# Batch normalisation on one core: the stream of 8 MB tiles moves from two hardware DMA queues to GpSimd's one software queue, one packet per DMA engine

## The chip, the cores and the metric

The kernel runs on one core of a Trainium2 chip. The metric is the device time of one launch in microseconds (us): the median of the runs was 2484.65 us. The core has a vector engine (VectorE, "DVE" in the profile), a scalar engine (ScalarE, "ACT"), GpSimd ("POOL"), TensorE (not used here) and SyncE ("SP"). Data moves between the device memory and the on-chip memory by DMA; the core has 16 DMA engines, and each transfer here is shared out over all of them.

## The reference

The input x has shape 32 x 256 x 128 x 128 in 32-bit floats (537 MB). Each channel is scaled and shifted with its own four parameters:

```python
def reference(x, gamma, beta, running_mean, running_var):
    eps = 1e-5
    mean = running_mean.reshape(1, -1, 1, 1)
    var = running_var.reshape(1, -1, 1, 1)
    gamma = gamma.reshape(1, -1, 1, 1)
    beta = beta.reshape(1, -1, 1, 1)
    return gamma * (x - mean) / np.sqrt(var + eps) + beta
```

So every element is read once, multiplied by a number of its channel, added to another, and written once.

## The kernel before

The 256 channels are two blocks of 128, one channel to a partition. With 32 images this gives 64 tiles (NT), each of 128 partitions x 16384 floats: 128 rows of 65,536 bytes, 8 MB in all. Three buffers of that size (NBUF = 3) hold tiles in turn: tile i is loaded into buffer i mod 3, worked on in place, and stored from there.

**Head.** SP issues the left half of tile 0 (L88), then four small broadcast loads with the parameters (L91), then the right half of tile 0 (L95), then the whole tiles from 1 on (L102). VectorE and ScalarE turn the parameters into one scale and one shift for each channel (L107 to L125).

**A tile's work.** VectorE takes columns 0 to 14335 of a tile in two instructions (2560 columns, then 11776, both L130) and counts each in the semaphore `vdone`; ScalarE takes the last 2048 columns (L141) and counts in `adone`. Tile 0 is cut at its half instead, so that VectorE can begin when the left half is there. In the last tile ScalarE takes 7168 columns, so that both engines end sooner.

**Order of transfers.** Loads are issued by SP and go to one hardware queue, q1; stores are issued by ScalarE (L154) and go to another, q10. From tile 3 on, SP waits until the earlier store out of the same buffer has landed (`stored`, L101) and until VectorE has done the first piece of the tile before (`vdone`, the wait on L102). ScalarE issues the store of tile i behind its own part of tile i, and begins its part only when VectorE is done with tile i (L162) and the store of tile i - 1 has landed (L165). So at most one store is under way until near the end, while a load runs beside it. Each transfer has its own semaphore per buffer (`loaded`, `stored`), which rises by 16, one for each DMA engine.

**End.** SP waits for the last store of each buffer (L172).

Of the kernel before, what the change touches and what calls it, by code (L numbers as in the profile page):

```python
# [8 lines left out]
NBUF = 3  # L9
# [3 lines left out]
VCOLS = 14336  # L13
VLAST = 9216


@with_exitstack
def kernel(
    ctx: ExitStack,
    tc: tile.TileContext,  # L20
    x: bass.AP,
    gamma: bass.AP,
    beta: bass.AP,
    running_mean: bass.AP,
    running_var: bass.AP,
    out: bass.AP,
):
    nc = tc.nc
    eps = 1e-5
    f32 = mybir.dt.float32  # L30

    N, C, H, W = x.shape
    P = nc.NUM_PARTITIONS
    assert C % P == 0
    NCB = C // P
    HW = H * W
    NT = N * NCB
    B = 32
    NQ = P // B
    NE = 16  # L40
    NPAR = 4

    xr = x.rearrange("n (cb p) h w -> (n cb) p (h w)", p=P)
    outr = out.rearrange("n (cb p) h w -> (n cb) p (h w)", p=P)

    params = ctx.enter_context(tc.tile_pool(name="params", bufs=1))
    data = ctx.enter_context(tc.tile_pool(name="data", bufs=1))
    bufs = [data.tile([P, HW], f32, name=f"t{s}", tag=f"t{s}") for s in range(NBUF)]
    rows = params.tile([B, NPAR * C], f32, name="rows", tag="rows")
    turned = params.tile([B, NPAR * C], f32, name="turned", tag="turned")  # L50
    par = params.tile([P, NPAR, NCB], f32, name="par", tag="par")
    eps_t = params.tile([P, 1], f32, name="eps_t", tag="eps")
    std_t = params.tile([P, NCB], f32, name="std_t", tag="std")
    rstd_t = params.tile([P, NCB], f32, name="rstd_t", tag="rstd")
    scale_t = params.tile([P, NCB], f32, name="scale_t", tag="scale")
    ms_t = params.tile([P, NCB], f32, name="ms_t", tag="ms")
    shift_t = params.tile([P, NCB], f32, name="shift_t", tag="shift")

    loaded = [tc.alloc_semaphore(f"loaded{s}") for s in range(NBUF)]
    stored = [tc.alloc_semaphore(f"stored{s}") for s in range(NBUF)]
    early = tc.alloc_semaphore("early")
    vdone = tc.alloc_semaphore("vdone")
    adone = tc.alloc_semaphore("adone")
    fetched = tc.alloc_semaphore("fetched")
    vec = tc.alloc_semaphore("vec")
    act = tc.alloc_semaphore("act")

    with tc.tile_critical():  # L70
        count = [0]

        def step(inst, sem=None, value=None):

            if sem is not None:
                inst._wait_ge(sem, value)
            elif count[0]:
                inst._wait_ge(vec, count[0])
            inst.then_inc(vec, 1)
            count[0] += 1  # L80
            return count[0]

        left, right = slice(0, HW // 2), slice(HW // 2, HW)
        last = NT - 1

        nc.sync.dma_start(out=bufs[0][:, left], in_=xr[0][:, left]).then_inc(early, 16)  # L88
        zeroed = step(nc.vector.memset(rows[:], 0.0))  # L89
        for r, ap in enumerate((running_var, gamma, beta, running_mean)):  # L90
            inst = nc.sync.dma_start(out=rows[0:NE, r * C : (r + 1) * C], in_=ap.partition_broadcast(NE))  # L91
            if r == 0:
                inst._wait_ge(vec, zeroed)
            inst.then_inc(fetched, 16)
        nc.sync.dma_start(out=bufs[0][:, right], in_=xr[0][:, right]).then_inc(loaded[0], 16)  # L95
        for i in range(1, NT):
            s, turn = i % NBUF, i // NBUF


            if turn:  # L100
                nc.sync.wait_ge(stored[s], 16 * turn)  # L101
            inst = nc.sync.dma_start(out=bufs[s][:], in_=xr[i]).then_inc(loaded[s], 16)  # L102
            if turn:
                inst._wait_ge(vdone, 2 * (i - 1) + 1)


        step(nc.vector.memset(eps_t[:], eps))  # L107
        step(nc.vector.transpose(out=turned[:], in_=rows[:]), fetched, 16 * NPAR)  # L108

        blocks = turned.rearrange("p (rc q b) -> p rc q b", q=NQ, b=B)  # L110
        flat = par.rearrange("p r cb -> p (r cb)")
        for q in range(NQ):
            placed = step(nc.vector.tensor_copy(out=flat[q * B : (q + 1) * B], in_=blocks[:, :, q, 0]))  # L113
        var_t, gamma_t, beta_t, mean_t = (par[:, r] for r in range(NPAR))
        nc.scalar.activation(  # L115
            out=std_t[:],
            in_=var_t,
            func=mybir.ActivationFunctionType.Sqrt,
            bias=eps_t[:],
            scale=1.0,  # L120
        )._wait_ge(vec, placed).then_inc(act, 1)
        step(nc.vector.reciprocal(out=rstd_t[:], in_=std_t[:]), act, 1)  # L122
        step(nc.vector.tensor_mul(out=scale_t[:], in0=gamma_t, in1=rstd_t[:]))  # L123
        step(nc.vector.tensor_mul(out=ms_t[:], in0=mean_t, in1=scale_t[:]))  # L124
        ready = step(nc.vector.tensor_sub(out=shift_t[:], in0=beta_t, in1=ms_t[:]))  # L125
        nc.vector.wait_ge(vec, ready)

        def vector_part(i, first, end):
            t, cb = bufs[i % NBUF], i % NCB
            return nc.vector.tensor_scalar(  # L130
                out=t[:, first:end],
                in0=t[:, first:end],
                scalar1=scale_t[:, cb : cb + 1],
                scalar2=shift_t[:, cb : cb + 1],
                op0=mybir.AluOpType.mult,
                op1=mybir.AluOpType.add,
            ).then_inc(vdone, 1)

        def scalar_part(i, first):
            t, cb = bufs[i % NBUF], i % NCB  # L140
            return nc.scalar.activation(  # L141
                out=t[:, first:],
                in_=t[:, first:],
                func=mybir.ActivationFunctionType.Identity,
                bias=shift_t[:, cb : cb + 1],
                scale=scale_t[:, cb : cb + 1],
            ).then_inc(adone, 1)

        def landed(i):
            return loaded[i % NBUF], 16 * (i // NBUF + 1)  # L150

        def store(i):
            s = i % NBUF
            nc.scalar.dma_start(out=outr[i], in_=bufs[s][:])._wait_ge(adone, i + 1).then_inc(stored[s], 16)  # L154

        vector_part(0, 0, HW // 2)._wait_ge(early, 16)
        vector_part(0, HW // 2, VCOLS)._wait_ge(*landed(0))
        for i in range(1, NT):
            vector_part(i, 0, STEP)._wait_ge(*landed(i))
            vector_part(i, STEP, VLAST if i == last else VCOLS)  # L160
        for i in range(last):
            nc.scalar.wait_ge(vdone, 2 * (i + 1))  # L162
            inst = scalar_part(i, VCOLS)
            if i:
                inst._wait_ge(stored[(i - 1) % NBUF], 16 * ((i - 1) // NBUF + 1))  # L165
            store(i)
        scalar_part(last, VLAST)._wait_ge(*landed(last))
        nc.scalar.wait_ge(vdone, 2 * NT)
        store(last)

        for s in range(NBUF):
            nc.sync.wait_ge(stored[s], 16 * ((NT - s + NBUF - 1) // NBUF))  # L172


# [28 lines left out]
```

## Time and profile before

| quantity | value |
|---|---|
| median of 3 runs | 2484.65 us (2484.54 to 2486.47) |
| span of the profiled execution | 2483.3 us |
| VectorE busy | 508.8 us (20%) |
| ScalarE busy | 139.8 us (6%) |
| GpSimd busy | 0.2 us |
| read from and written to device memory | 536.94 MB and 536.87 MB |
| mean rate over the span | 432 GB/s |
| load of a whole tile, issue to landing (median) | 37.0 us |
| store of a whole tile, issue to landing (median) | 36.5 us |

The time of the runs is taken from outside the program, the span from its first to its last instruction; the difference is about 1.3 us. The instructions that issue DMAs or wait on semaphores are not counted as busy, so GpSimd, SP and most of ScalarE's work with queues is seen in the waits and in the timeline, not in the busy times. "Packets" are the pieces in which a DMA engine moves data: before, each row of a tile is one packet of 65,536 bytes, and each engine closes a transfer with a packet of 4 bytes that raises the semaphore.

### The profile page before, as it was taken

The numbers are of one execution on the slowest core, as the hardware profiler recorded it, in microseconds if no ns is written. First come the engines' busy times: TensorE is split into PE (matmuls) and PEld (weight loads), VectorE is DVE, ScalarE is ACT, GpSimd is POOL, SyncE is SP. The second block draws the span as 40 slices with busy tenths as digits, with TensorE's granted clock in tenths as the row PEclk, the third lists the DMA queues.
The fourth block names the chain that finished last, engine by engine and source line by source line (L and its number), as shares of the span: only waits on it lengthen the run. The fifth ranks groups of instructions, "written<-read, shape, count | busy, mean of one in ns | idle before, by whom it ended". The sixth has DMA issues, their size and how long they took to land.

```text
span 2483.3 us, 516 instructions
## 1 busy us (share of the span) xinstructions
DVE 508.8 (20%) x139; ACT 139.8 (6%) x66; POOL 0.2 (0%) x4
## 2 busy tenths in 40 slices
DVE  3122121221212212122121221212212122121220
ACT  0000000000000000000000000000000000000001
POOL 0000000000000000000000000000000000000000
DMA  9999999999999999999999999999999999999999
GB/s 415 430 439 434 428 436 436 435 433 430 432 433 438 430 432 433 435 424 437 437 428 436 438 436 429 437 435 430 436 437 436 430 437 435 429 437 435 433 433 408
DMA packets 18708, 1073.85 MB, mean 432 GB/s; under 512 B 2128, under 2 KB 2192, under 8 KB 2192
## 3 DMA queue, kind: packets, MB, share of 16 engines
q1 hardware_dynamic: 9488, 536.94, 50.1%
q10 hardware_dynamic: 9216, 536.88, 49.9%
q14 instruction: 4, 0.03, 0.0%
HBM read 536.94 MB, written 536.87 MB: 432 GB/s over the span
## 4 chain that ended last, share of the span: by engine, by line
DMA 93%; DVE 4%; another core or an unknown queue 1%; ACT 0%; issue 0%; SPq 0%; DVEq 0%
DMA t<-in_x_dram 93%; DVE t L130 4%; ACT t L141 0%; SPq L91 0%; DVE rows L89 0%; SPq L95 0%; DVE eps_t L107 0%; DVEq L198 0%; SPq L70 0%
## 5 line engine op out<-in xcount | busy, mean ns | idle before, releaser
L130 DVE TENSOR_SCALAR t<-t,scale_t,shift_t 128x11776 f32<-128x11776 f32 (+2 forms) x128 | 505.3, 3989 | 1930.4 <-DMA t<-in_x_dram 1930.2
L141 ACT ACTIVATE t<-t,shift_t,scale_t 128x2048 f32<-128x2048 f32 x64 | 138.2, 2159 | 2299.3 <-DMA out_dram<-t 2276.6
L108 DVE STREAM_TRANSPOSE turned<-rows 32x1024 f32<-32x1024 f32 x1 | 1.2, 1233 | 12.5 <-DMA rows<-in_running_mean_dram 12.5
L115 ACT ACT_TABLE_LOAD x1 | 1.3, 1283 | 0.9 <-SPq L70 0.9
L89 DVE MEMSET rows<- 32x1024 f32 x1 | 0.9, 912 | 1.2 <-SPq L70 1.2
L115 ACT ACTIVATE std_t<-par,eps_t 128x2 f32<-128x2 f32 x1 | 0.3, 296 | 14.7 <-DVE par L113 14.7
L113 DVE COPY par<-turned 32x8 f32<-32x8 f32 x4 | 0.6, 161 | 0.1
L122 DVE RECIPROCAL rstd_t<-std_t 128x2 f32<-128x2 f32 x1 | 0.2, 166 | 0.4 <-ACT std_t L115 0.4
L125 DVE TENSOR_TENSOR shift_t<-par,ms_t 128x2 f32<-128x2 f32 x1 | 0.2, 161 | 0.0
L124 DVE TENSOR_TENSOR ms_t<-par,scale_t 128x2 f32<-128x2 f32 x1 | 0.2, 161 | 0.0
L123 DVE TENSOR_TENSOR scale_t<-par,rstd_t 128x2 f32<-128x2 f32 x1 | 0.2, 160 | 0.0
L187 POOL MEMSET const-bfloat16-1.0<- 128x1 bf16 x1 | 0.1, 101 | 0.0
L187 POOL MEMSET const-uint8-127<- 128x1 uint8 x1 | 0.1, 101 | 0.0
L187 POOL MEMSET const-float32-0.0<- 128x1 f32 x1 | 0.1, 98 | 0.2 <-issue 0.2
L187 POOL MEMSET const-float32-1.0<- 128x1 f32 x1 | 0.1, 98 | 0.0
L107 DVE MEMSET eps_t<- 128x1 f32 x1 | 0.1, 59 | 0.1
## 6 DMA issues: line engine op xcount, KB each, us to landing
t<-in_x_dram SPq DMA_DIRECT2D x2, 4096.0 KB, 16.5
out_dram<-t ACTq DMA_DIRECT2D x64, 36.5
t<-in_x_dram SPq DMA_DIRECT2D x63, 37.0
rows<-in_running_var_dram SPq DMA_DIRECT2D x1, 16.0 KB, 11.3
rows<-in_gamma_dram SPq DMA_DIRECT2D x1, 16.0 KB, 11.1
rows<-in_beta_dram SPq DMA_DIRECT2D x1, 16.0 KB, 10.9
rows<-in_running_mean_dram SPq DMA_DIRECT2D x1, 16.0 KB, 11.3
```

Of the source, the lines that this page charges most:

```text
L89: zeroed = step(nc.vector.memset(rows[:], 0.0))
L107: step(nc.vector.memset(eps_t[:], eps))
L108: step(nc.vector.transpose(out=turned[:], in_=rows[:]), fetched, 16 * NPAR)
L113: placed = step(nc.vector.tensor_copy(out=flat[q * B : (q + 1) * B], in_=blocks[:, :, q, 0]))
L115: nc.scalar.activation(out=std_t[:], in_=var_t, func=mybir.ActivationFunctionType.Sqrt, bias=eps_t[:], scale=1.0,)._wait_ge(vec, placed).t ...
L122: step(nc.vector.reciprocal(out=rstd_t[:], in_=std_t[:]), act, 1)
L123: step(nc.vector.tensor_mul(out=scale_t[:], in0=gamma_t, in1=rstd_t[:]))
L124: step(nc.vector.tensor_mul(out=ms_t[:], in0=mean_t, in1=scale_t[:]))
L125: ready = step(nc.vector.tensor_sub(out=shift_t[:], in0=beta_t, in1=ms_t[:]))
L130: return nc.vector.tensor_scalar(out=t[:, first:end], in0=t[:, first:end], scalar1=scale_t[:, cb : cb + 1], scalar2=shift_t[:, cb : cb + 1 ...
L141: return nc.scalar.activation(out=t[:, first:], in_=t[:, first:], func=mybir.ActivationFunctionType.Identity, bias=shift_t[:, cb : cb + 1] ...
L187: nc = _bacc.Bacc("TRN2", target_bir_lowering=False, num_devices=1)
```

## The change

The two halves of tile 0 and the parameters stay on SP's queue. All other loads and all stores are issued by GpSimd, in the order: load 1, store 0, load 2, store 1, load 3, store 2, load 4 and so on. GpSimd's DMAs go to its one software queue, for which GpSimd itself writes the descriptors. With `single_packet=True` the eight rows that each DMA engine moves of a tile form one packet.

A store waits in GpSimd's queue for both parts of the work on its tile (`vdone` and `adone`). A load into a buffer used before waits for the store out of that buffer (`stored`). SP no longer waits for the work of VectorE, and ScalarE neither issues stores nor waits for VectorE or for an earlier store: it begins its part of a tile when the tile has landed. The right half of tile 0 has a semaphore of its own, `first`, so the counts of `loaded[0]` begin with tile 3. ScalarE gets one wait for the scale and shift, and the last waits move from SP to GpSimd.

```diff
-        nc.sync.dma_start(out=bufs[0][:, right], in_=xr[0][:, right]).then_inc(loaded[0], 16)
-        for i in range(1, NT):
+        nc.sync.dma_start(out=bufs[0][:, right], in_=xr[0][:, right]).then_inc(first, 16)
+
+        def load(i):
             s, turn = i % NBUF, i // NBUF
+            inst = nc.gpsimd.dma_start(out=bufs[s][:], in_=xr[i], single_packet=True).then_inc(loaded[s], 16)
             if turn:
-                nc.sync.wait_ge(stored[s], 16 * turn)
-            inst = nc.sync.dma_start(out=bufs[s][:], in_=xr[i]).then_inc(loaded[s], 16)
-            if turn:
-                inst._wait_ge(vdone, 2 * (i - 1) + 1)
+                inst._wait_ge(stored[s], 16 * turn)
+
+        def store(i):
+            s = i % NBUF
+            nc.gpsimd.wait_ge(vdone, 2 * (i + 1))
+            inst = nc.gpsimd.dma_start(out=outr[i], in_=bufs[s][:], single_packet=True)
+            inst._wait_ge(adone, i + 1).then_inc(stored[s], 16)
+
+        load(1)
+        for i in range(NT):
+            store(i)
+            if i + 2 < NT:
+                load(i + 2)
...
         nc.vector.wait_ge(vec, ready)
+        nc.scalar.wait_ge(vec, ready)
...
         def landed(i):
-            return loaded[i % NBUF], 16 * (i // NBUF + 1)
-
-        def store(i):
-            s = i % NBUF
-            nc.scalar.dma_start(out=outr[i], in_=bufs[s][:])._wait_ge(adone, i + 1).then_inc(stored[s], 16)
+            if i == 0:
+                return first, 16
+            return loaded[i % NBUF], 16 * (i // NBUF + (1 if i % NBUF else 0))
...
-        for i in range(last):
-            nc.scalar.wait_ge(vdone, 2 * (i + 1))
-            inst = scalar_part(i, VCOLS)
-            if i:
-                inst._wait_ge(stored[(i - 1) % NBUF], 16 * ((i - 1) // NBUF + 1))
-            store(i)
-        scalar_part(last, VLAST)._wait_ge(*landed(last))
-        nc.scalar.wait_ge(vdone, 2 * NT)
-        store(last)
+        for i in range(NT):
+            scalar_part(i, VLAST if i == last else VCOLS)._wait_ge(*landed(i))
 
         for s in range(NBUF):
-            nc.sync.wait_ge(stored[s], 16 * ((NT - s + NBUF - 1) // NBUF))
+            nc.gpsimd.wait_ge(stored[s], 16 * ((NT - s + NBUF - 1) // NBUF))
```

## The prediction

> **What bounds the kernel now.** First the page: the busy times, the DMA row, the queues and the chain that ended last.
>
> ```profile
> span 2483.3 us, 516 instructions
> ...
> DVE 508.8 (20%) x139; ACT 139.8 (6%) x66; POOL 0.2 (0%) x4
> ...
> DMA  9999999999999999999999999999999999999999
> ...
> q1 hardware_dynamic: 9488, 536.94, 50.1%
> q10 hardware_dynamic: 9216, 536.88, 49.9%
> ...
> DMA 93%; DVE 4%; another core or an unknown queue 1%; ACT 0%; issue 0%; SPq 0%; DVEq 0%
> ```
>
> No engine is busy over 20%, and the two queues' packets together fill 100.0% of the 16 DMA engines' span: the DMA engines are the bound. Next, three stretches cut out of the trace (length; busy VectorE, ScalarE and GpSimd; clock; DMA share; GB/s): loads alone in the head, 56 tiles in the middle, and the end, where mostly stores are left.
>
> ```profile
> 1.95:22.40 20.45, 7.12 (x12) 0.53 (x2) 0.00 (x0) 1.00 1.02 417
> ...
> 244.99:2408.90 2163.91, 442.74 (x111) 117.18 (x56) 0.00 (x0) 1.00 1.00 434
> ...
> 2441.87:2461.20 19.33, 5.27 (x2) 6.36 (x1) 0.00 (x0) 1.00 1.00 434
> ```
>
> The middle takes 2163.91/56 = 38.64 us for a load and a store, 16.777 MB, so 434 GB/s, 19.3 us for each transfer; the end has the same rate. The DMA share is 1.00 in all three: a queue alone keeps the engines as full as two do. Then the waits of SP's queue, and the head in order of time.
>
> ```profile
> SPq L101 <- DMA out_dram<-t: 1398.1, 61, 68.8
> SPq L102 <- DVE t L130: 985.0, 61, 16.2
> ```
>
> ```profile
> 18.04 4.55 DVE L130 TENSOR_SCALAR t<-t,scale_t,shift_t 128x8192 f32<-128x8192 f32 x1
> 23.85 3.48 DVE L130 TENSOR_SCALAR t<-t,scale_t,shift_t 128x6144 f32<-128x6144 f32 x1 [1.27 <-DMA t<-in_x_dram]
> 27.36 2.09 ACT L141 ACTIVATE t<-t,shift_t,scale_t 128x2048 f32<-128x2048 f32 x1 [10.23 <-DVE t L130]
> 29.49 0.37 ACTq L154 DMA_DIRECT2D out_dram<-t  x1
> 54.40 7.93 DVE L130 TENSOR_SCALAR t<-t,scale_t,shift_t 128x2560 f32<-128x2560 f32 x2 [27.07 <-DMA t<-in_x_dram]
> ```
>
> SP waits 2383.1 us in all, yet no DMA engine runs dry: those waits cost nothing, and dropping them gains nothing. In the head, tile 0 is worked on from 18.04 to 29.45 us while loads 1 and 2 keep the DMA engines full.
>
> So only three things can change the time: the cost of a packet, a hole in the DMA engines' work, and the cost of passing from one transfer to the next.
>
> **Packets, a gain.** The trace's records of single packets last 2.418 us for 65,536 bytes, 1.213 us for 32,768, 0.046 us for 1,024 and 0.009 us for 4. The first two differ by 1.205 us, so the bytes of a row take 2.410 us and 0.008 us is the packet's own. Successive records of an engine overlap by 0.004 us (a row begins every 2.414 us), so what a packet costs the engine is nearer 0.004 us. One packet for eight rows removes 7 of 8 in 63 loads and 64 stores: 127 x 7 = 889 per engine. At 0.004 us that is 3.6 us, at 0.008 us 7.1 us; if the price belongs to the row and not to the packet, nothing. I take 3.6, by the spacing, which is what fills the span. More than this can't come of it: a row's bytes keep their 2.410 us.
>
> **The steady state, nothing.** In the new order a store sits on the software queue ahead of the next load, so the two take turns, 19.3 us each. When load i lands, store i-1 starts. The work on tile i takes 8.0 us (54.40 to 62.33), so store i enters the queue 11 us before store i-1 ends, and behind it load i+1 is there already for another 19.3 us. Load i+2 waits for store i-1 and is queued behind store i in GpSimd's order; it is issued some 36 us before its turn. Every wait in GpSimd's order is over in time, so issue and description of a transfer are hidden unless they take over 11 us; the only rows are 0.34 us (SP and ScalarE issuing) and, as the other end, the 8.0 us for which VectorE works. Without that cover the price would be the excess times 64. Changing direction costs nothing in the rows: from 60 us on the records of each engine alternate between q1 and q10 at the same 2.414 us.
>
> **Taken away, nothing.** 63 loads, 64 stores and their waits leave SP's and ScalarE's queues. ScalarE's part now runs beside VectorE's, 2.09 us inside 8.0. At the end load 63, store 62 and store 63 follow each other; the last work (6.36 us, L141) lies under store 62 (19.3 us), as it lies under DMA now. The last waits only change engine.
>
> **The head, a loss.** Before, tile 0, load 1 and load 2 were on one queue in that order. Now load 2 is behind store 0 in GpSimd's queue, and load 1 starts beside tile 0 as a second queue. If an engine, once it has taken up load 1's packet, keeps to it for its eight rows, tile 0's rest comes after it, and by 2 + 2 x 19.3 + about 0.4 for the parameters = 41 us both are in and the queues are empty. Then come 0.5 us from the last packet of the right half to VectorE's start (23.35 to 23.85 before), 3.48 us for VectorE's second piece, and 1.0 us from an issue to its first packet (0.95 to 1.95 us for L88): 5.0 us. Row by row in turns, the halves of tile 0 also come last and the hole is the same. The parameters come later, but their work and VectorE's first piece (4.55 us) fit under the right half (9.6 us).
> One thing makes it longer. Load 1 is already there, so VectorE goes straight on to tile 1, 1.61 and 6.41 us, while GpSimd is to write the descriptors of store 0. No row shows GpSimd doing that beside VectorE. Bounds: no delay, 5.0; delay until VectorE has done both pieces, 13.0. I take a delay of the first piece, 1.6: 6.6 us, as GpSimd is ready before the second starts. The low end of the hole is 0: tile 0 complete before load 1's packets begin.
> The Trainium skill, page "SBUF — State Buffer", section "Who interferes with whom", speaks against the change here: an instruction of VectorE that streams through two ports locks GpSimd out for its whole length, and descriptors of GpSimd's DMAs are then late. The row that bears on it is L130's two shapes, 9216 columns more in 4.795 us, 0.52 ns a column. By the rule the hole would be the one of 6.6 or 13.0, by the plain rows 5.0.
>
> **From one transfer to the next, unknown.** Where one queue works alone (q1 at 23 us, between tile 0 and load 1; q10 at 2461 us, between the last two stores), the next row's record starts 6 ns after the 4-byte record that ends a transfer, with no gap: so 0 per boundary. The upper end is the largest stall that the trace has when a new transfer joins: at 32 us, when the first store starts, the load rows under way grow from 2.42 to between 2.74 and 3.64 us, some 0.8 us per engine (12.6 us summed over 16); over 127 boundaries 102 us. I take 0, as both queues of before showed it.
> The skill's page "DMA: Bandwidth & Descriptors", section "Anatomy of one DMA — SWDGE (gpsimd) path", gives each software DMA about 2.0 us beyond its bytes. If none of that overlapped, an estimate by that page is 127 x 2.0 = 254 us more; the records above say that for a hardware queue it overlaps wholly, and no run here shows the software queue.
>
> **Sum.** 2483.3 - 3.6 + 6.6 = 2486.3 us of span; the runs' median is 1.35 above the span, so 2487.7 us.
>
> **Rivals.**
> 1. VectorE holds up store 0 for both its pieces: hole 13.0, time 2484.65 - 3.6 + 13.0 = 2494.1. For it: the two instructions follow each other at 0.03 us. Against: GpSimd waits already when the first ends. It decides from a hole of 8.6 us.
> 2. Each boundary on the single queue costs something, since the same queue has to read, write and report with no second queue to fill in. From 2487.7, 2.0 us more (16 ns per boundary) make the kernel slower than the bound of measurement; 0.1 us each give 2500.4, 0.8 us 2589. For it: nothing covers it. Against: the records of 6 ns.
> 3. Faster: no hole, because tile 0 is through first, and 0.008 us per packet: 2484.65 - 7.1 = 2477.5; if the extra that load rows show over 2.418 us (64 us over 16 engines, 4.0 each, nearly all before 1141 us) also went as loads no longer meet stores, 2473.5. For it: the stores show almost no such extra. Against: both come late in the same mix with the same packets, so it isn't the mix.
> 4. The packets aren't merged: gain 0, 2491.3. Against: nothing in the trace speaks to it.
>
> **Chances.** A measurement of this kernel can tell about 0.2%, 5.0 us, from no change: 2479.7 to 2489.6. Forecast 0.35, with a range of its own of 2481 to 2489.6; rival 1 0.22, rival 2 0.18, rival 3 0.20, rival 4 0.05. Faster 0.20, same 0.35, slower 0.22 + 0.18 + 0.05 = 0.45. The range 2475 to 2505 leaves out a little of rival 3 and of rival 2 what lies above 0.14 us per boundary, some 0.15 in all.
>
> **What will show it.** Packets: 16 large ones per DMA transfer instead of 128, near 19.28 us each. Steady state: 38.58 us per tile, DMA share 1.00, GpSimd waiting for VectorE and for stores without gaps. Head: a DMA share near 0 for some 5 to 13 us from about 41 us, with store 0 issued after it and VectorE's tile 1 in the same stretch. If the share is below 1.00 in the middle, the boundary rival holds; a period over 38.64 us makes the prediction wrong, as does a head without the hole.

## The result, and the profile after

The changed kernel takes 2499.56 us (2498.44 to 2500.20) against 2485.52 us (2484.54 to 2486.47) for the kernel before in the same runs: 14.0 us or 0.58% longer, ratio 1.0058 with a 95% interval of 1.0046 to 1.0070. The forecast was 2487.7 us and no change that can be measured; the range of 2475 to 2505 holds the time. The span of the profiled execution is 2496.7 us, 13.3 us longer than before.

The page of the changed kernel: busy times, DMA row, queues, the chain that ended last, and the groups of GpSimd's issues (count, then busy time and mean duration).

```profile
span 2496.7 us, 460 instructions
...
DVE 508.7 (20%) x139; ACT 139.8 (6%) x66; POOL 74.5 (3%) x131
...
DMA  8999999999999999999999999999999999999998
...
q0 software_dynamic: 18288, 1065.36, 98.7%
q1 hardware_dynamic: 416, 8.45, 0.8%
...
another core or an unknown queue 90%; ACT 5%; DMA 3%; DVE 0%; issue 0%; POOL 0%; SPq 0%; DVEq 0%; POOLq 0%
...
L107 POOL DMA_DIRECT2D out_dram<-t x64 | 34.6, 541 | 1738.9 <-DVE t L140 1672.6
L100 POOL DMA_DIRECT2D t<-in_x_dram x63 | 39.6, 629 | 648.9 <-DMA out_dram<-t 647.9
```

The DMA engines are still the bound: both end slices of the DMA row are below 9, the 38 between are full. The software queue's 18288 packets are 16256 rows of 65,536 bytes and 2032 closing ones of 4 bytes, so each row is still a record of its own: the eight rows of an engine did not form one packet, against the title and the section on the change. One issue takes GpSimd some 0.54 us, hidden behind transfers of 19.3 us. The chain calls 90% of the span an unknown queue: most of the software queue's transfers get no name there, so this view tells nothing of the change, and the stretches and the timeline have to.

Three stretches of the changed kernel (columns as before: length; busy VectorE, ScalarE, GpSimd; clock; DMA share; GB/s): a gap in the head, 31 tiles in the middle, and the early part.

```profile
42.40:48.20 5.80, 5.39 (x3) 4.08 (x2) 1.32 (x2) 1.00 0.00 0
...
1218.93:2416.70 1197.77, 246.00 (x62) 64.94 (x31) 33.12 (x62) 1.00 1.00 434
140.00:600.00 460.00, 88.18 (x23) 23.93 (x12) 12.28 (x23) 1.00 1.00 432
```

In the head all 16 DMA engines stand still for these 5.8 us (0.00). The middle runs at 1197.77/31 = 38.64 us per tile, the same as before to the last digit. The early part is a little slower than the middle (432 against 434 GB/s; the kernel before has 433 in the same stretch). The timeline shows what happens in the gap (start, duration).

```profile
42.81 11.33 DVE L140 TENSOR_SCALAR t<-t,scale_t,shift_t 128x6144 f32<-128x6144 f32 x3 [1.38 <-DMA t<-in_x_dram]
46.88 1.06 POOL L107 DMA_DIRECT2D out_dram<-t  x1 [44.71 <-DVE t L140]
47.92 6.33 POOL L100 DMA_DIRECT2D t<-in_x_dram  x1
54.69 0.53 POOL L107 DMA_DIRECT2D out_dram<-t  x1 [0.44 <-issue]
```

The last data of tile 0 arrive at 42.3 us; VectorE's second piece lasts from 42.81 to 46.29, GpSimd begins store 0 at 46.88 and ends its issue at 47.94, and the store's first row starts at 48.5. Nothing else was queued in the meantime.

With the trace's records of single DMA packets the 13.3 us can be split fully. For each profile the table takes, per DMA engine (mean over 16): time without a packet in the head, the time by which rows last longer than 2.418 us, the time between an engine's own last packet and the last of all, and the time from that one to the end of the span. Two kernels of the experiments stand beside.

| us per DMA engine | before | changed | same order, hardware queue | loads 1 and 2 on SP's queue |
|---|---|---|---|---|
| no packet, up to 30 us | 0.2 | 0.3 | 0.2 | 0.3 |
| no packet, hole in the head | 0 | 6.5 | 0 | 0 |
| rows longer than 2.418 us | 4.1 | 7.5 | 4.2 | 4.2 |
| engines not ending together | 1.3 | 3.2 | 3.9 | 5.6 |
| last packet to end of span | 1.6 | 3.1 | 2.1 | 2.9 |
| sum over "before" | | 13.4 | 3.2 | 5.8 |
| span over "before" | | 13.3 | 3.1 | 5.8 |

The sums match the spans. In the changed kernel 109 of the 120 us of extra row time (summed over 16 engines) lie on the eighth row of a transfer: 96 on the eighth rows of loads, where an engine passes from a load to a store, and 13 on the eighth row of the first store, at 65 us, where it passes on to load 2. The eighth rows of all later stores have next to nothing. The two first passages, at 65 and 85 us, cost 0.8 and 1.0 us per engine (rows of up to 3.5 and 3.9 us), the next ones from a load to a store 0.1 to 0.4 us; from 1000 us on some 0.03 us are left on average.

### The profile page after: what moved, and what is told of

It reads as the page before. It is cut to its first block, busy times and chain, and to the rows that moved or that the text cites. A ratio compares the mean times of both kernels' runs of the same rounds, so it can differ in the third digit from the quotient of the medians.

```text
span 2496.7 us, 460 instructions
## 1 busy us (share of the span) xinstructions
DVE 508.7 (20%) x139; ACT 139.8 (6%) x66; POOL 74.5 (3%) x131
## 3 DMA queue, kind: packets, MB, share of 16 engines
q0 software_dynamic: 18288, 1065.36, 98.7%
## 4 chain that ended last, share of the span: by engine, by line
another core or an unknown queue 90%; ACT 5%; DMA 3%; DVE 0%; issue 0%; POOL 0%; SPq 0%; DVEq 0%; POOLq 0%
ACT t L151 5%; DMA t<-in_x_dram 3%; DVE t L140 0%; POOL out_dram L107 0%; SPq L92 0%; DVE rows L90 0%; DVE eps_t L116 0%; DVEq L199 0%; POOLq L106 0%; SPq L71 0%
## 5 line engine op out<-in xcount | busy, mean ns | idle before, releaser
L107 POOL DMA_DIRECT2D out_dram<-t x64 | 34.6, 541 | 1738.9 <-DVE t L140 1672.6
L100 POOL DMA_DIRECT2D t<-in_x_dram x63 | 39.6, 629 | 648.9 <-DMA out_dram<-t 647.9
```

What stands on the lines that cost most here:

```text
L100: inst = nc.gpsimd.dma_start(out=bufs[s][:], in_=xr[i], single_packet=True).then_inc(loaded[s], 16)
L107: inst = nc.gpsimd.dma_start(out=outr[i], in_=bufs[s][:], single_packet=True)
```

## The experiments

**The flag off.** `single_packet=True` is dropped in both calls:

```diff
-            inst = nc.gpsimd.dma_start(out=bufs[s][:], in_=xr[i], single_packet=True).then_inc(loaded[s], 16)
+            inst = nc.gpsimd.dma_start(out=bufs[s][:], in_=xr[i]).then_inc(loaded[s], 16)
...
-            inst = nc.gpsimd.dma_start(out=outr[i], in_=bufs[s][:], single_packet=True)
+            inst = nc.gpsimd.dma_start(out=outr[i], in_=bufs[s][:])
```

> The changed kernel without single_packet. Theory from the profile after: the flag does nothing for rows of 65,536 bytes, since they begin every 2.414 us there as before; time as the changed kernel, 2499.6 (2498.4 to 2500.2), the same 16256 rows on the software queue. Rival, the flag does save its 3.6 us and something else ate them: 2503. Rival, the flag costs (the last row of a transfer is stretched because a whole packet has to be closed): 2490 to 2496, with the long last rows gone.

Measured: 2499.44 us, ratio 1.0061 (1.0049 to 1.0074), the same queue row of 18288 packets, the same hole (6.4 us) and 6.3 us of extra row time. The flag does nothing that can be seen here.

**Load 2 ahead of store 0.**

```diff
         load(1)
+        load(2)
         for i in range(NT):
             store(i)
-            if i + 2 < NT:
+            if 0 < i < NT - 2:
```

> Load 2 is issued ahead of store 0, all else as in the changed kernel. Theory: the DMA engines' hole from 41.9 to 48.2 us goes, as 19.3 us of load 2 lie behind tile 0 and load 1; 6.5 us less, 2493.1, and a time of load 2's issue near 0.6 us in place of 6.33, since VectorE is idle then. Rival, the hole is only moved (store 0 and load 3 come late later on): 2499.6. Rival, the engines' common start after the hole also brings the long last rows of loads: 2489.

Measured: 2500.35 us, ratio 1.0062 (1.0049 to 1.0075). The theory fell: the hole didn't go, it moved, from 42 to 48 us to 62 to 68 us. Its stretches:

```profile
60.00:62.00 2.00, 0.00 (x0) 0.00 (x0) 0.00 (x0) 1.00 0.61 262
62.00:68.00 6.00, 5.67 (x3) 5.67 (x3) 1.05 (x1) 1.00 0.00 0
```

The packet records of one DMA engine say why (start in us, queue, bytes; q1 is SP's, q0 the software queue). The records name no engine; this one is followed from the end of each record to the record that starts there.

```
 6.23 q0 65536    8.64 q1 32768    9.85 q0 65536   12.26 q1 32768   13.47 q0 65536
...
26.76 q0 65536   29.18 q1  1024   29.22 q0 65536   31.64 q1     4   31.64 q0     4
31.65 q1  1024   31.69 q0 65536   34.23 q1     4   34.24 q0 65536   36.66 q1  1024
36.71 q0 65536   39.29 q1     4   39.29 q0 65536   41.71 q1  1024   41.76 q0 65536
44.33 q1     4   44.34 q0 65536   46.76 q1 32768
```

The engine takes one record from each queue in turn, however short it is. Each 1 KB of the parameters, and each 4 bytes that close one, waits for a row of 64 KB to pass (2.42 to 2.59 us here). So the longer the software queue is filled, the later tile 0 comes: it's always the last of what was queued at the start, and the 3.5 us of work on its right half and GpSimd's issue are uncovered. In the changed kernel it shows in the DMA issues (last column: us from issue to landing; before, the first parameter row took 11.3 and tile 0's halves 16.5):

```profile
t<-in_x_dram SPq DMA_DIRECT2D x2, 4096.0 KB, 32.7
...
rows<-in_running_var_dram SPq DMA_DIRECT2D x1, 16.0 KB, 30.7
```

**Loads 1 and 2 back on SP's queue**, behind tile 0, all else on GpSimd's (the semaphores `ahead`, and the waits on them, are left out here):

```diff
+            if i < 3:
+                nc.sync.dma_start(out=bufs[s][:], in_=xr[i]).then_inc(ahead[i - 1], 16)
+                return
             inst = nc.gpsimd.dma_start(out=bufs[s][:], in_=xr[i], single_packet=True).then_inc(loaded[s], 16)
```

> Loads 1 and 2 stay on SP's hardware queue behind tile 0, as before the change; from store 0 and load 3 on GpSimd's queue with the flag. Theory: no hole, as in the run with load 2 first: 2493, and tile 0 is worked on from 18 us. If the run with load 2 first loses its hole and this one doesn't fall too, the head isn't the cause. Store 0 is described while VectorE is at work or idle, covered by loads 1 and 2 either way.

Measured: 2491.58 us (2490.85 to 2492.57), ratio 1.0029 (1.0017 to 1.0040). This takes the hole out, as the stretches show, the first where the changed kernel had its hole, the second where it lay with load 2 ahead (a packet counts where it starts, so a DMA share can be off by a few hundredths):

```profile
24.00:60.00 36.00, 7.22 (x3) 3.86 (x2) 0.67 (x1) 1.00 1.02 433
60.00:80.00 20.00, 3.86 (x1) 0.00 (x0) 1.08 (x2) 1.00 0.98 423
```

8.0 us of the runs' time are gone, and 7.6 us of the profiled span: the hole's 6.5, 3.3 of extra row time and 0.2 at the end, less 2.4 that the engines end further apart. The kernels that had the hole, four profiles, show 5.9 to 7.5 us of extra row time, the two here without it 4.2: after the hole all engines start a store within 0.2 us of each other, and their first changes of direction are the dear ones. Whether the common start is what makes them dear, the experiment with the engines set apart asks.

**The same order on SP's hardware queue.** All of GpSimd's DMAs and waits are issued by SP instead, without the flag (`nc.gpsimd` becomes `nc.sync` in `load`, `store` and the last waits).

> The same order of transfers as in the changed kernel, all on SP's hardware queue, no flag. No hole in the head, as load 1 lies behind tile 0 there. Theory A, the long last rows of loads belong to the order (every engine changes from load to store at the same time): they stay, 3 to 5 us, and with the software queue's longer end (1.4 us) gone the time is 2488 to 2490. Theory B, they belong to the software queue: 2484 to 2486, as the kernel before.

Measured: 2488.19 us (2486.90 to 2491.23), ratio 1.0016 (1.0008 to 1.0025). Theory A's time, but not by its sum: the extra of the rows is 4.2 us, as before, only now it lies on the eighth rows and unevenly on the engines, so they end 3.9 us apart on average instead of 1.3. So of the change's 14.0 us, the order on one queue is worth 4.0 and the software queue, with its head, the rest.

**VectorE held while GpSimd describes.** VectorE's work on tile 1 waits for a one-column memset that GpSimd issues behind store 0 and load 2 (the semaphore `go` and the tile `mark` are new).

```diff
+            if i == 0:
+                nc.gpsimd.memset(mark[:], 0.0).then_inc(go, 1)
...
+        nc.vector.wait_ge(go, 1)
         for i in range(1, NT):
```

> The changed kernel, but VectorE begins tile 1 only when GpSimd has issued store 0 and load 2 (a one-column memset on GpSimd gives the sign). Theory, VectorE keeps GpSimd from writing descriptors while it works: store 0's issue falls from 1.06 to some 0.55 us and load 2's from 6.33 to 0.55; the hole in the head is 0.5 us shorter, 5.9 to 6.0; time within 1 of the changed kernel. Rival, the first DMAs after a pause are slow by themselves: 1.06 and 6.33 stay.

Measured: 2499.58 us in one run, and this timeline:

```profile
47.17 0.53 POOL L109 DMA_DIRECT2D out_dram<-t  x1 [45.01 <-DVE t L144]
47.69 0.54 POOL L102 DMA_DIRECT2D t<-in_x_dram  x1
48.22 0.12 POOL L118 MEMSET mark<- 128x1 f32 x1
48.44 7.93 DVE L144 TENSOR_SCALAR t<-t,scale_t,shift_t 128x2560 f32<-128x2560 f32 x2 [1.86 <-POOL mark L118]
```

1.06 and 6.33 us became 0.53 and 0.54: VectorE's work is what kept GpSimd from finishing. In the changed kernel the 6.33 us end at 54.25, 0.11 us after VectorE's (54.14). The hole shrinks by 0.4 us (6.5 to 6.0), as only the wait of store 0 lies in it; load 2 has 19.3 us of store 0 as cover. The Trainium skill, page "SBUF — State Buffer", describes this lock (section "Who interferes with whom"); its "DVE-end + ~115 ns" (section "A bandwidth-pool intuition that's wrong (but worth ruling out)") agrees with the 0.11 us here.

**Short pieces, with the flag and without.** Each tile goes in two DMAs of every other 8 KB piece of its rows. The loads are shown; the stores are cut in the same way, and the counts that are waited for double:

```diff
+    def cut(ap, b):
+        return ap.rearrange("p (a b c) -> p b a c", a=4, b=2)[:, b]
...
+            for b in range(2):
+                inst = nc.gpsimd.dma_start(out=cut(bufs[s][:], b), in_=cut(xr[i], b), single_packet=True)
+                inst.then_inc(loaded[s], 16)
```

> The changed kernel with each tile moved by two DMAs of every other 8 KB piece of its rows: 32 pieces of 8 KB for each DMA engine and DMA, with the flag. Theory: one record per piece still, each costing some 4 ns beyond its bytes; 2 x 127 x 32 - 127 x 8 = 7112 pieces more per engine, 28 us, and 127 more closing records, 1 us: 2528, and the same time without the flag. Rival, the flag joins the pieces where they are short: 2500 with it, 2528 without.

> The same 8 KB pieces without the flag. Theory: 2528, as with it. Rival: 2528 against 2500 with it.

Measured: 2530.32 us with the flag and 2530.47 without, both at ratio 1.0183 (1.0168 to 1.0198). The queue row of the page with the flag:

```profile
q0 software_dynamic: 134112, 1065.37, 99.8%
```

134112 packets are 130048 pieces and 4064 closing ones: nothing is joined. The pieces begin every 305.9 ns, the rows of 65,536 bytes every 2414.3; the difference of 57,344 bytes takes 2108.4 ns, so a packet costs 305.9 - 8192 x 2108.4/57344 = 4.7 ns beyond its bytes. That price is real, but this flag doesn't save it, neither here nor with rows of 64 KB.

**The last store on SP's queue**, added to the kernel with loads 1 and 2 there (SP's wait for `final` is left out):

```diff
+            if i == last:
+                nc.sync.wait_ge(vdone, 2 * NT)
+                nc.sync.dma_start(out=outr[i], in_=bufs[s][:])._wait_ge(adone, NT).then_inc(final, 16)
+                return
```

> Loads 1 and 2 on SP's queue as in the earlier run, and the last store too (tile 63), all between them on GpSimd's queue. Theory: the software queue's end is longer (2.9 us from the last packet to the end of the span against 1.6 before), so 1.3 us go: 2490.3 against 2491.6. On its own queue the last store also begins beside store 62, row by row, which changes no sum. Rival, the longer end belongs to the order or to the core's own end: 2491.6.

Measured: 2491.16 us (2489.68 to 2492.90), ratio 1.0028 (1.0017 to 1.0040), against 1.0029 without. In its profile 3.0 us pass from the last packet to the end, as many as with the software queue's own last store (2.9). The theory fell: the longer end is not the last store's queue. It appears in the profiles where GpSimd issued DMAs; what of it is GpSimd's stays open.

**The DMA engines set apart.** To the kernel with the changed order on the hardware queue two loads are added that only some engines move; their data are overwritten by load 2, which waits for both (not shown).

```diff
+        nc.sync.dma_start(out=bufs[2][0:8], in_=xr[0][0:8]).then_inc(apart, 16)
+        nc.sync.dma_start(out=bufs[2][8:12, left], in_=xr[0][8:12, left]).then_inc(apart, 16)
```

> All transfers on SP's hardware queue in the changed order, and two extra loads ahead of load 1 that only some of the DMA engines have to move: 64 KB on eight of them (2.4 us) and 32 KB on four of those (1.2 us). They set the engines apart by up to 3.6 us. Theory: the long last rows of loads come from all engines changing direction in step; set apart, the extra of the rows falls from 4.2 us per engine (mean) to under 2, and the time stays within 2 of the run without them, 2486 to 2490, although the slowest engine has 3.6 us more to move. Rival, the extra has another source (time since the start, addresses): it stays near 4.2 and the time rises by 3 to 4: 2491 to 2492.

Measured: 2494.84 us, ratio 1.0039 (1.0025 to 1.0053). The time is outside both forecasts, but the rows answer. The extra loads were themselves dear: their rows, and those beside them, took 7.9 to 9.2 us instead of 2.42, 9.0 us extra per engine up to 41 us. After that the extra is 0.3 us per engine for the rest of the run, where the same order without them has 3.7. At 75 us the first and the last engine close a transfer 4.5 us apart; without the extra loads it is 0.5 us at 62 us. The early stretch of both kernels, first without, then with the engines apart:

```profile
140.00:600.00 460.00, 95.21 (x24) 25.13 (x12) 0.00 (x0) 1.00 1.00 432
```

```profile
140.00:600.00 460.00, 91.49 (x25) 25.14 (x12) 0.00 (x0) 1.00 1.00 434
```

Two more kernels tried to gain from that with gentler offsets of 1.2 and 2.4 us (32 KB to every fourth partition, for eight engines and then for four), one in the changed order on SP's queue and one in the kernel before.

```diff
+        nc.sync.dma_start(out=bufs[2][0:32:4, left], in_=xr[1][0:32:4, left]).then_inc(apart, 16)
+        nc.sync.dma_start(out=bufs[2][0:16:4, right], in_=xr[1][0:16:4, right]).then_inc(apart, 16)
```

> As the run with the DMA engines set apart (all on SP's hardware queue, changed order), but the extra loads go to every fourth partition, 32 KB on eight engines and 32 KB on four of those, so that no long rows arise from the extra loads themselves (they were 8 to 9 us each there). Theory: 1.2 and 2.4 us of offset; if that is enough, the rows' extra falls from 4.2 us per engine to under 2, and the slowest engine gives 2.4 for it: 2484 to 2487, against 2488.2 in that order without. Rival, only offsets of 5 us and more help: extra near 4, time 2489 to 2491.

> The kernel before with the same two extra loads. Theory: its rows' extra (4.1 us per engine, 5.4 on the slowest) falls under 2, at a price of 2.4: 2482 to 2485, no slower than before. Rival: extra stays, 2486 to 2488.

Measured: 2488.82 us, ratio 1.0018 (1.0009 to 1.0026), extra 2.8 us per engine instead of 4.2; and 2487.88 us, ratio 1.0017 (1.0008 to 1.0026), extra 5.3 instead of 4.1. The first falls by a third and pays as much for the offset; the second doesn't fall. So long rows go with engines in step in the one-queue order (9.0 us of disturbance removed nearly all, 1.2 to 2.4 us a third), while for the two queues of before the cause is open. The distance alone doesn't decide: the changed kernel's engines were 3.5 to 4.9 us apart between 365 and 559 us, as far as these, and its rows still had 1.6 us of extra per engine between 300 and 600 us. Which engines have to be apart, and why, no run shows. No version beat the kernel before.

## Why the prediction was right in its range and wrong in its middle

Forecast and measurement differ by 2499.56 - 2487.7 = 11.9 us. By the steps of the prediction:

- *What bounds the kernel*, and *the steady state, nothing*: right. DMA share 1.00 and 38.64 us per tile in both kernels; GpSimd's waits and issues (0.54 us) are hidden.
- *Packets, a gain* of 3.6 us: this step failed. Its price per packet was good (4 ns; 4.7 measured), its premise was not: the records stay one per row, with the flag or without, and the queues take turns by rows. So its 3.6 us were never there. The rival "the packets aren't merged" was given 0.05 as there was nothing against the premise in the trace of before; it holds.
- *The head, a loss* of 6.6 us: right in mechanism and place. That the size was met too (6.5) is luck, as its parts were off in ways that cancel: VectorE delayed store 0 by 0.5 us, not 1.6; but from VectorE's end to the first row there are 0.59 us until GpSimd begins, 0.53 of issue and 0.57 until the row, 1.7 in all, where 1.0 was taken from the hardware queue. The rival with 13.0 us fell, since the long wait (6.33) hit load 2, which has cover.
- *From one transfer to the next*, taken as 0: this step failed too. It was read from two places where a queue did the same direction twice (load after load, store after store); a load's last row before a store was not among them. The sentence on the steady state, that changing direction costs nothing in the rows from 60 us on, holds for most rows only: in the kernel before, the load rows after 60 us exceed 2.418 us by 50.7 us in all, summed over 16 engines; rival 3 counts this within its 64 us. The rows' extra rose by 3.4 us per engine, 27 ns per boundary, and the engines ended 1.9 us further apart. The rival of a cost per boundary, which was to decide from 16 ns, was right in kind, though the cost isn't steady but falls from 1.0 us to some 0.03 us.
- *Taken away, nothing*: the end of the span came 1.4 us later after the last packet, which was not in the sum.
- *Sum*: 3.6 + 3.4 + 1.9 + 1.4 make 10.3 of the 11.9 us. The rest is 0.1 in the first 30 us and 1.5 by which the runs' median stands further above this span (2.9 us) than before (1.35), as the profiled execution was the shortest of the four, less 0.1 in the head. The forecast "no change" came from letting an unsupported gain cancel a well-read loss: without the gain the same sum gives 2491.3, slower. The time lies in the range of 2475 to 2505 because the range is wide: it is outside the 2479.7 to 2489.6 that the prediction called no change. Rivals 2 (a cost per boundary) and 4 (no gain) came in part together, and the chances had weighed each by itself.

## What to carry to other kernels

Where the DMA engines are as full as here and rows are 64 KB, another queue gave nothing in the middle, and a longer packet would have little to give (4.7 ns of 2414 for each row); what can change is a hole, so ask of every new queue what it puts beside the first transfers that others wait for. Short transfers that start the work belong alone at the front: beside a second queue of long rows each short packet waits one long row. A price of 0 read between two equal transfers says nothing of the passage from one direction to the other.

## What the runs showed of the hardware

- The software queue's first DMA is slow to start: GpSimd ended load 1's issue at 2.16 us, its first row came at 6.26; with the engines idle, store 0's first row came 0.57 us after its issue.
- With all transfers on one queue, a row that precedes a change from load to store lasts up to 3.9 us instead of 2.42 while the 16 engines change within about 0.5 us of each other (so did, once, the row before the first change from store to load, up to 3.5 us). It has nearly its normal length once they have drifted 7.0 us apart, from about 950 us on in the changed kernel.
- Eight rows of 64 KB into eight neighbouring partitions took 7.9 to 9.2 us each, and rows of the other engines at the same time as well; the 32 KB rows to every fourth partition took their normal 1.21 us.
